# Moving mixer A's heads up behind their query jobs, and gathering the products with the values of mixers B and C

## The chip, the cores and the metric

One core of a Trainium2 chip runs the whole program. The metric is the device time of one execution in microseconds; the kernel before takes 1936.8 us (median of 3 runs, 1934.24 to 1936.91).

## The reference, cut to what matters

Two layers run over two sequences with shared weights, a "prompt" of 512 tokens (p) and a "sample" of 1024 tokens (s), all float32, 1024 channels:

```
even layer:  h = rmsnorm(x)*(1+scale)+shift;  q,k,v,gates = split(h @ w_in_ab)
  A: 8 query heads on 2 key heads, RMS norm and rotary on q and k, dense softmax over all keys
  B: 8 heads, softmax over three dilated sliding windows, mixed by their log-sum-exp
  x += gate * rmsnorm(concat(A*silu(ga), B*silu(gb)) @ w_out_ab)
odd layer:   the same frame around w_in_cd, w_out_cd
  C: 12 heads, each query sees a window of 8 x 16 neighbours on a 64-wide grid, learned bias
  D: a real 2-D Fourier transform and a linear map
```

## The kernel before, in words

The sequences are cut into units of 512 tokens: the sample has units 0 and 1, the prompt unit 2. A layer's input projection is split into jobs of 256 columns. For layer 0 they are, in order, `kva` (keys and values of A), `qa0`, `qa1` (queries of A's heads 0 to 3 and 4 to 7), `kb0`, `qb0`, `vb0`, `kb1`, `qb1`, `vb1` (mixer B), and four gate jobs `ga0` to `gb1` (list in `run`, line 1271). A job multiplies in three float32r passes (high and low halves), norms and rotates on VectorE, ScalarE and GpSimd, and leaves a closure `finish` in `self.late`; `flush` runs it in the middle of a later job: 4 transposes on TensorE for each 128 columns, then a spill to DRAM (`q0s`, `k0s`). The attention functions load queries, keys and values back from DRAM. All DMAs are issued on one queue, that of SyncE (SP), which issues in order.

The line order of the program is only a priority. The program is built with a planner (`schedule_with_timeline_sim=True`, line 1396) that lists the instructions of each engine in an order of its own, by an estimate of when each is ready. So the projection's matrix products of later jobs fill in where attention waits. That order is then fixed: on the chip every engine runs its list in order.

Mixer A (`attn_a`, L683) runs for one key head, 4 query heads, at a time. In the kernel before both calls stand after job `kb0` (lines 1300 to 1303). With the first of them `self.idle` turns false, and from then on the `finish` transposes take their PSUM bank from the three of the projections (`pD`) instead of the two that attention transposes into (`pT`).

Mixer B works on pairs of heads (`attn_b_pair`, L768) for 512 queries: four softmax steps for both heads, then `out_b` (L821) for each head. Mixer C works on one head and 512 queries (`attn_c_unit`, L1049) in four windows. Each head's end in B and C is a *unit* here, and has the same pieces: transposes of the probabilities on TensorE into a `pT` bank (L147), a copy of the bank to SBUF (`copy_pt`, L664, in turn on ScalarE and VectorE, into two tags of two buffers, so four copies can be held), and products with the values (`pv2`, L670), which take 64 of the array's columns: product number n writes the upper or the lower half of the bank `po`, by n odd or even. `fold` adds the halves. In the kernel before each bank's products follow its copy in program order.

- C, sample: 24 units of 4 banks, 3 products each; C, prompt: 12 units of 4 banks, 2 products each.
- B, sample: 16 units with banks of 3, 3, 4, 4 products; B, prompt: 8 units with 3, 3, 4.

A float32 product is recorded as two matmuls, so that C of the sample has 24 x 12 x 2 = 576 records.

Of the kernel before, what the change touches and what calls it, by code (L numbers as in the profile page):

```python
# [18 lines left out]
P = 128  # L19
# [103 lines left out]
class Body:  # L123
# [537 lines left out]
    def copy_pt(self, pt, nm, w=512, rows=P):  # L661
        self.np += 1
        t = self.sb.tile([P, 512], F32, tag="pt" + "hl"[self.np % 2], name="ptc" + nm, bufs=PTB)
        (self.nc.vector.tensor_copy if self.np % PTD == 0 else self.nc.scalar.copy)(t[:rows, :w], pt[:rows, :w])  # L664
        return t

    def pv2(self, out, v, p, n):

        x = 64 * (n % 2)
        self.nc.tensor.matmul(out[x:x + HD], v, p, start=n < 2, stop=False, tile_position=(0, x), skip_group_check=True)  # L670

    def fold(self, po, nm, w=512, view=None):

# [147 lines left out]
    def out_b(self, g, h, pr, x, ev, V1, V2, nm):  # L821
        hf = g.hf
        po = self.pO(f"o{nm}")

        for gi in range(2):
            pt = self.pT(f"pt1{nm}{gi}")
            for i, (t, j) in enumerate(((0, 0), (0, 1), (1, 0), (1, 1))):
                self.tr(pt[:, i * P:(i + 1) * P], ev[2 * gi + t][:, j * P:(j + 1) * P])
            ph = self.copy_pt(pt, f"1{nm}{gi}")
            for j, t, cnt, b in ((0, 0, 1, 0), (1, 0, 2, 1), (2, 1, 1, 3)):  # L830
                t += 2 * gi
                self.pv2(po[:, t * P:(t + cnt) * P], V1[2 * gi + j], ph[:, b * P:(b + cnt) * P], j if gi == 0 else 2 + j)

        pc = po.rearrange("p (t r a) -> p r t a", t=4, r=4)
        for kt in range(hf):
            pt = self.pT(f"pt2{nm}{kt}")
            for t in range(4):
                self.tr(pt[:, t * P:(t + 1) * P], ev[t][:, 256 + kt * P:256 + (kt + 1) * P])
            p2 = self.copy_pt(pt, f"2{nm}{kt}").rearrange("p (t r a) -> p r t a", t=4, r=4)
            for r in range(4):  # L840
                self.pv2(pc[:, r], V2[r * hf + kt], p2[:, r], 2 + r)
        of = self.fold(po, nm, view=lambda v: v.rearrange("p (t r a) -> p r t a", t=4, r=4))
        self.dma(self.md[0, g.name, pr][HD * x:HD * x + HD, 512 * h:512 * h + 512], of)

# [204 lines left out]
    def attn_c_unit(self, g, h, head):  # L1049

        nc, pool = self.nc, self.sb
        n, S, nh = g.name, g.S, g.nhalf
        nrow = 12 if nh == 2 else 8
        NG = nrow // 4
        pr, hh = head // 2, head % 2
        nm = f"c{n}{head}{h}"

        T = self.l1.tile([P, nrow, 32], F32, tag="bt", name="T" + nm, bufs=2)
        r0 = 1 + 4 * h if nh == 2 else 5
        src = self.bias_dr[:, head, r0:r0 + nrow, :]  # L1060
        self.dma(T, bass.AP(src.tensor, src.offset, [[32, 8], [NCH * 24 * 32, 16], [1, 32 * nrow]]))
        T = T[:, ::-1, :]
        K0 = 4 * h * GRID
        ksrc = self.kd[1, n, pr][:, :, K0:K0 + nrow * GRID]
        km = self.load_k(ksrc, HD * hh, nrow * GRID, nm, *((self.l1, "kc") if hh else ()))
        q = self.load_q(self.qd[1, n, pr], HD * hh, h, nm)
        if hh == 0:
            vsrc = self.vd[1, n, head // 4][pr % 2]
            self.vt = []
            for i in range(4):  # L1070
                c0, c1 = max(16 * i - 8, 0), min(16 * i + 24, GRID)
                V = pool.tile([P, NG, P], F32, tag="V", name=f"V{nm}{i}", bufs=VB)
                self.dma(V[0:4 * (c1 - c0)], vsrc[:, c0:c1, h:h + NG].rearrange("r c g d -> r c (g d)"))
                self.vt.append(V)
        Vs = [V[:, :, HD * hh:HD * hh + HD] for V in self.vt]
        if nh == 2:
            TT = self.l1.tile([P, nrow, 32], F32, tag="btr", name="TT" + nm, bufs=1)
            nc.gpsimd.tensor_add(TT, T, self.mrow[:, h, :].unsqueeze(2).to_broadcast([P, nrow, 32]))
            T = TT
        bias = {}  # L1080
        for kind, wo, w in ((0, 8, 24), (1, 0, 32), (2, 0, 24)):
            b = self.l1.tile([P, nrow, w], F32, tag="bias", name=f"bi{nm}{kind}", bufs=BB)
            nc.gpsimd.tensor_add(b, T[:, :, wo:wo + w], self.mcol[:, kind, wo:wo + w].unsqueeze(1).to_broadcast([P, nrow, w]))  # L1083
            bias[kind] = b
        po = self.pO("o" + nm)
        k3 = km.rearrange("p (r c) -> p r c", c=GRID)
        for i in range(4):
            c0, c1 = max(16 * i - 8, 0), min(16 * i + 24, GRID)
            w = c1 - c0
            W, kw = nrow * w, 4 * w  # L1090
            b = bias[(0, 1, 1, 2)[i]]
            e = pool.tile([P, 1024], F32, tag="e", name=f"e{nm}{i}", bufs=EB)[:, 0:W]
            ps = self.pS(f"s{nm}{i}")[:, 0:W]
            self.qk(ps.rearrange("p (r c) -> p r c", c=w), q, slice(P * i, P * i + P), k3[:, :, c0:c1])
            m = pool.tile([P, 1], F32, tag="nmax", name=f"m{nm}{i}", bufs=4)
            nc.vector.tensor_tensor_reduce(out=e, in0=ps, in1=b.rearrange("p r w -> p (r w)"), scale=1.0,  # L1096
                                           scalar=-3.0e38, op0=ALU.add, op1=ALU.max, accum_out=m)
            ngm = pool.tile([P, 1], F32, tag="nmx2", name=f"ngm{nm}{i}", bufs=4)
            nc.vector.tensor_scalar_mul(ngm, m, -0.125)  # L1099
            den = pool.tile([P, 1], F32, tag="den", name=f"den{nm}{i}", bufs=4)  # L1100
            nc.scalar.activation(e, e, AF.Exp, bias=ngm, scale=0.125, accum_out=den)  # L1101
            rd = pool.tile([P, 1], F32, tag="rd", name=f"rd{nm}{i}", bufs=4)
            nc.vector.reciprocal(rd, den)
            nc.vector.tensor_scalar_mul(e, e, rd)
            pt = self.pT(f"pt{nm}{i}")
            for x in range(NG):
                self.tr(pt[:kw, x * P:(x + 1) * P], e[:, x * kw:(x + 1) * kw])
            ph = self.copy_pt(pt, f"{nm}{i}", NG * P, kw)
            for x in range(NG):
                self.pv2(po[:, i * P:(i + 1) * P], Vs[i][:kw, x], ph[:kw, x * P:(x + 1) * P], NG * i + x)  # L1110
        self.dma(self.md[1, n, pr][HD * hh:HD * hh + HD, 512 * h:512 * h + 512], self.fold(po, nm))


# [111 lines left out]
    def run(self):  # L1225
# [4 lines left out]
        with tc.tile_pool(name="l0", bufs=1) as self.l0:  # L1230
# [42 lines left out]
            for g, us in ((gp, [2]), (gs, [0, 1])):  # L1273
                done = []
                if g is gs:
                    self.idle = True
                    done = jobs[3:3 + LEAD0 + LEAD1]
                    for i, kind in enumerate(done[:LEAD0]):
                        if i == SO:
                            H = self.s3_operand(0, 2)  # L1280
                        self.s2_0_job(Hs, [0], kind)
                    self.bias_shift()
                    self.s3(0, 2, "e", H)
                    Hs[1], step = self.s1_steps(0, 1)
                    for kind, i in zip(done[LEAD0:], ST0):
                        step(i[0])
                        self.s2_0_job(Hs, [0], kind)
                        step(i[1])
                for kind in jobs:
                    if g is gp and kind == "ga0":  # L1290
                        Hs[0] = self.s1(0, 0)
                    self.s2_0_job(Hs, [1] if kind in done else us, kind)
                    m = mods.pop(0) if mods else None
                    if end:
                        end()
                    end = self.adaln(*m) if m else None
                    if g is gp and kind == "qa1":
                        self.mb = self.l0.tile([P, 1248], F32, name="mask_b", tag="mask", bufs=1)
                        self.dma(self.mb, self.a["mask_b"])
                    if kind == "kb0":  # L1300
                        self.idle = False
                        self.attn_a(g, 0)
                        self.attn_a(g, 1)
                    elif kind == "vb0":
                        self.attn_b(g, 0, 0)
                    elif kind == "vb1":
                        self.attn_b(g, 0, 1)
                        if g is gs:
                            self.attn_b(g, 1, 0)
                            self.attn_b(g, 1, 1)  # L1310
# [89 lines left out]
```

## Time and profile before

| what | value |
|---|---|
| runs | 1936.8, 1936.91, 1934.24 us |
| the profiled execution | 1936.24 us, its span 1934.2 us |
| TensorE busy | 1857.0 us (96%) |
| VectorE, ScalarE, GpSimd busy | 1195.3, 927.1, 591.4 us |
| granted TensorE clock, mean | 0.988 |

The span is the time from the first to the last instruction; 2 us of the execution lie around it. A matmul's end is modelled and matmuls overlap, so a busy share near 100% does not show how closely they follow one another: the distance from one start to the next does. The stages on the span, read from which matmuls run when: layer 0 of the prompt to 310 us, projections of the sample with little attention from 310 to 520, mixer A of the sample from 520 to 960 and its mixer B to 1228, layer 1 with C of the prompt from 1365 and C of the sample from 1485 to 1820, then the last output projection.

### The profile page before, as it was taken

To read this page: it belongs to the slowest core of one execution; us is meant where nothing else is said; L and a number is where in the kernel's file an instruction comes from. 1 tells how busy PE (TensorE), PEld (TensorE's weight loads), DVE (VectorE), ACT (ScalarE), POOL (GpSimd) and SP (SyncE) were. 2 spreads that over 40 slices of the span, in tenths; PEclk is the share of its full clock that TensorE was granted. 3 is DMA by queue.
4 is the path that set the end of the run, shared out by engine and by line. 5 is a ranking of instruction groups with operands and counts; after the bars stand their busy time and mean duration, and the time that the engine had idled before them with its cause. 6 is when DMAs were issued, how large, how long until landed. Compare 5 with 4: busy or idle time off the path is not lost. (4 is left out here: it accounts for less than half of the span.)

```text
span 1934.2 us, 37850 instructions
## 1 busy us (share of the span) xinstructions
PE 1857.0 (96%) x13752; PEld 1614.9 (83%) x13752; DVE 1195.3 (62%) x3110; ACT 927.1 (48%) x2197; POOL 591.4 (31%) x534
## 2 busy tenths in 40 slices
PE   6999999999999999999999989799999999998998
PEld 4789768999998988889977667788887888887898
DVE  2688863254767666767765677564566544668733
ACT  3456543343356554555554555453554433445531
POOL 3631224354722121121101121353433323335310
PEclk9999999999999999999999999899999999999999
DMA  9754445467763323244344563654677664668643
GB/s 303 253 175 147 126 138 184 126 197 224 231 207 112 104 93 108 64 135 145 116 146 150 182 193 113 205 181 136 216 233 224 195 180 150 200 206 267 221 156 142
DMA packets 255353, 333.03 MB, mean 172 GB/s; under 512 B 25672, under 2 KB 172456, under 8 KB 255168
## 3 DMA queue, kind: packets, MB, share of 16 engines
q1 hardware_dynamic: 255168, 330.62, 54.4%
q8 instruction: 108, 1.77, 0.4%
q14 instruction: 77, 0.63, 0.1%
HBM read 248.68 MB, written 81.87 MB: 171 GB/s over the span
## 5 line engine op out<-in xcount | busy, mean ns | idle before, releaser
L143 PE MATMUL y<-who,hhm 128*128 128x256 f32 x768 | 219.9, 288 | 13.0 <-ACT hhm L891 13.0
L143 PE MATMUL y<-who,hlm 128*128 128x256 f32 x768 | 218.6, 288 | 2.9 <-DVE hlm L892 2.9
L143 PE MATMUL y<-wlo,hhm 128*128 128x256 f32 x768 | 218.6, 287 | 0.2 <-DVE wlo L386 0.2
L143 PEld LDWEIGHTS y<-who,hhm 128*128 128x128 f32 x768 | 148.1, 193 | 16.6 <-ACT hhm L891 14.1
L143 PEld LDWEIGHTS y<-who,hlm 128*128 128x128 f32 x768 | 147.6, 193 | 5.4 <-DVE hlm L892 3.9
L143 PEld LDWEIGHTS y<-wlo,hhm 128*128 128x128 f32 x768 | 148.2, 194 | 1.8 <-issue 1.4
L717 ACT ACTIVATE eas<-sas,nmas 128x512 f32<-128x512 f32 x128 | 86.8, 684 | 69.9 <-DVE nmas L713 69.6
L1083 POOL TENSOR_TENSOR bics<-TTcs,mkc 128x288 f32<-128x288 f32 (+1 forms) x72 | 65.5, 911 | 127.7 <-DVE mcs L1096 108.1
L654 DVE TENSOR_TENSOR ptlas<-ptas,pthas 128x512 fp32r<-128x512 f32 x128 | 85.7, 685 | 19.6 <-ACT pthas L652 18.8
L386 POOL TENSOR_TENSOR wlo<-wso,who 128x512 fp32r<-128x512 f32 x40 | 55.9, 1400 | 132.4 <-ACT who L385 106.5
L708 DVE TENSOR_REDUCE mxas<-sas 128x1 f32<-128x512 f32 x128 | 86.3, 683 | 12.7 <-PE sas L143 12.2
L652 ACT CAST pthas<-ptas 128x512 fp32r<-128x512 f32 x128 | 70.5, 590 | 29.1 <-PE ptas L147 25.7
L143 PE MATMUL t1v<-wh1v,hh 128*128 128x256 f32 x288 | 82.2, 286 | 0.0
L143 PE MATMUL t1v<-wh1v,hl 128*128 128x256 f32 x288 | 82.0, 285 | 0.0
L143 PE MATMUL t1v<-wl1v,hh 128*128 128x256 f32 x288 | 81.9, 285 | 0.0
L1101 ACT ACTIVATE ecs<-ecs,ngmcs 128x288 f32<-128x288 f32 (+1 forms) x96 | 54.8, 571 | 56.3 <-DVE ngmcs L1099 54.8
L914 ACT ACTIVATE ysq<-y 128x256 f32<-128x256 f32 x96 | 36.6, 382 | 87.7 <-PE y L143 70.6
L147 PE MATMUL ptas<-ident,eas 128*128 128x128 f32 x512 | 76.6, 273 | 0.3 <-DVE eas L725 0.3
L143 PE MATMUL oas<-pthas,Vas 128*128 128x256 f32 x256 | 68.9, 285 | 0.0
L143 PE MATMUL oas<-ptlas,Vas 128*128 128x256 f32 x256 | 68.5, 294 | 0.2 <-DVE ptlas L654 0.2
L891 ACT CAST hhm<-og 128x512 fp32r<-128x512 f32 x48 | 29.7, 619 | 75.4 <-POOL og L890 46.1
L385 ACT CAST who<-wso 128x512 fp32r<-128x512 f32 x80 | 48.7, 616 | 35.3 <-PE y L143 10.8
(628 smaller groups left out, 6317.2 us busy)
## 6 DMA issues: line engine op xcount, KB each, us to landing
wso<-w_out_ab SPq DMA_DIRECT2D x48, 256.0 KB
kcs<-k1s SPq DMA_DIRECT2D x24, 384.0 KB
wso<-w_out_cd SPq DMA_DIRECT2D x32, 256.0 KB
ws1k<-w_in_cd SPq DMA_DIRECT2D x28, 256.0 KB
wskb<-w_in_ab SPq DMA_DIRECT2D x24, 256.0 KB
wsqb<-w_in_ab SPq DMA_DIRECT2D x24, 256.0 KB
wsvb<-w_in_ab SPq DMA_DIRECT2D x24, 256.0 KB
ws1q<-w_in_cd SPq DMA_DIRECT2D x24, 256.0 KB
```

What stands on the lines that cost most here:

```text
L143: self.nc.tensor.matmul(out, l, r, start=start, stop=stop, skip_group_check=True)
L147: self.nc.tensor.transpose(out, in_, self.ident[:k, :k])
L385: nc.scalar.copy(hi, st)
L386: (nc.vector if c in dve else nc.gpsimd).tensor_sub(lo, st, hi)
L652: nc.scalar.copy(h[:rows, :w], pt[:rows, :w])
L654: nc.vector.tensor_sub(lo[:rows, :w], pt[:rows, :w], h[:rows, :w])
L708: nc.vector.tensor_reduce(mx[:, c:c + 1], ps, op=ALU.max, axis=AX.X, negate=True)
L717: nc.scalar.activation(e[:, 512 * c:512 * c + 512], pss[c], AF.Exp, bias=nmx, accum_out=den[:, c:c + 1])
L891: nc.scalar.copy(hh, t)
L914: nc.scalar.activation(sq[:, 0:256], ps[:, t], AF.Square, accum_out=ss[j][:, job:job + 1])
L1083: nc.gpsimd.tensor_add(b, T[:, :, wo:wo + w], self.mcol[:, kind, wo:wo + w].unsqueeze(1).to_broadcast([P, nrow, w]))
L1101: nc.scalar.activation(e, e, AF.Exp, bias=ngm, scale=0.125, accum_out=den)
```

## The change

Three edits. `attn_a(g, 0)` now follows job `qa0` and `attn_a(g, 1)` follows `qa1`, each behind a `flush` that runs the job's own `finish`; `self.idle` turns false after `qa0`. In `out_b` and `attn_c_unit` all transposes and copies of a unit come first, then all its products. `together` adds a wait of the first product for the last copy, and an order without a wait from each product to the next.

```diff
     def copy_pt(self, pt, nm, w=512, rows=P):
...
+        self.copied = (self.nc.vector.tensor_copy if self.np % PTD == 0 else self.nc.scalar.copy)(t[:rows, :w], pt[:rows, :w])
+    def together(self, ms):
+        self.after(ms[0], self.copied)
+        for a, b in zip(ms, ms[1:]):
+            self.after(b, a, False)
 # out_b
-            ph = self.copy_pt(pt, f"1{nm}{gi}")
-            for j, t, cnt, b in ((0, 0, 1, 0), (1, 0, 2, 1), (2, 1, 1, 3)):
-                t += 2 * gi
-                self.pv2(po[:, t * P:(t + cnt) * P], V1[2 * gi + j], ph[:, b * P:(b + cnt) * P], j if gi == 0 else 2 + j)
+            p1.append(self.copy_pt(pt, f"1{nm}{gi}"))
...
+        for gi in range(2):
+            for j, t, cnt, b in ((0, 0, 1, 0), (1, 0, 2, 1), (2, 1, 1, 3)):
+                t += 2 * gi
+                ms.append(self.pv2(...))
+        for kt in range(hf):
             for r in range(4):
-                self.pv2(pc[:, r], V2[r * hf + kt], p2[:, r], 2 + r)
+                ms.append(self.pv2(pc[:, r], V2[r * hf + kt], p2[kt][:, r], 2 + r))
+        self.together(ms)
 # attn_c_unit
-            ph = self.copy_pt(pt, f"{nm}{i}", NG * P, kw)
+            pts.append((self.copy_pt(pt, f"{nm}{i}", NG * P, kw), kw))
+        for i, (ph, kw) in enumerate(pts):
             for x in range(NG):
-                self.pv2(po[:, i * P:(i + 1) * P], Vs[i][:kw, x], ph[:kw, x * P:(x + 1) * P], NG * i + x)
+                ms.append(self.pv2(...))
+        self.together(ms)
 # run
-                    if kind == "kb0":
+                    if kind[:2] == "qa":
+                        self.flush()
                         self.idle = False
-                        self.attn_a(g, 0)
-                        self.attn_a(g, 1)
+                        self.attn_a(g, int(kind[2]))
```

## Rows read from the trace of the kernel before

**Rows 1.** The page, part 1: busy us, share of the span, instructions.
```profile
PE 1857.0 (96%) x13752; PEld 1614.9 (83%) x13752; DVE 1195.3 (62%) x3110; ACT 927.1 (48%) x2197; POOL 591.4 (31%) x534
```
**Rows 2.** Busy time by stage: PE, PEld, DVE, ACT, POOL, clock, DMA share, GB/s.
```profile
310.00:520.00 210.00, 208.07 (x1721) 201.28 (x1719) 100.18 (x217) 82.82 (x179) 107.04 (x84) 1.00 0.61 193
960.00:1100.00 140.00, 139.14 (x1131) 103.59 (x1129) 89.07 (x237) 68.88 (x150) 19.70 (x15) 1.00 0.49 154
1100.00:1228.00 128.00, 116.65 (x1135) 95.23 (x1135) 90.88 (x233) 62.72 (x152) 27.07 (x24) 0.97 0.54 163
1485.00:1742.00 257.00, 255.03 (x1712) 215.33 (x1711) 140.52 (x443) 104.14 (x253) 81.66 (x85) 1.00 0.64 191
1742.00:1820.00 78.00, 67.83 (x539) 60.36 (x540) 62.59 (x164) 42.59 (x112) 36.25 (x31) 0.93 0.78 246
```
**Rows 3.** The waits of PE from 1740 to 1820: total us, times, longest us.
```profile
PE ocs L670 <- ACT ptccs L664: 3.3, 1, 3.3
```
**Rows 4.** Timeline of PE: start us, us, instruction, merged count; two runs of products and what follows.
```profile
1401.11 0.44 PE L670 MATMUL ocp<-ptccp,Vcp 128*64 128x128 f32 x4
1401.48 0.42 PE L147 MATMUL ptcp<-ident,ecp 128*96 128x128 f32 x2
...
1659.98 0.88 PE L670 MATMUL ocs<-ptccs,Vcs 96*64 96x128 f32 x12
1660.79 0.66 PE L147 MATMUL ptcs<-ident,ecs 128*128 128x128 f32 x4
1661.20 0.42 PE L143 MATMUL scs<-kcs,qhcs 128*128 128x384 f32 x1
```
**Rows 5.** Timeline of PE: projections ahead of a run, and transposes that follow no run.
```profile
1665.35 0.40 PE L143 MATMUL c1g<-hh,wh1g 128*128 128x512 f32 x1
1665.58 0.40 PE L143 MATMUL c1g<-hl,wh1g 128*128 128x512 f32 x1
1665.90 0.88 PE L670 MATMUL ocs<-ptccs,Vcs 128*64 128x128 f32 x12
...
1220.96 0.60 PE L147 MATMUL pt2bs<-ident,ebs 128*128 128x128 f32 x4
1221.32 0.36 PE L143 MATMUL y<-who,hlm 128*128 128x256 f32 x1
```
**Rows 6.** The first and the last run of products on PE's timeline.
```profile
205.20 0.65 PE L670 MATMUL obp<-ptc1bp,V1bp 128*64 128x128 f32 x6
...
1819.90 0.65 PE L670 MATMUL ocs<-ptccs,Vcs 96*64 96x128 f32 x6
```
**Rows 7.** Busy time of L670 alone (PE, PEld), in three of these stages.
```profile
960.00:1100.00 140.00, 16.15 (x196) 11.80 (x196) 1.00 0.49 154
1100.00:1228.00 128.00, 20.51 (x252) 15.20 (x252) 0.97 0.54 163
1485.00:1742.00 257.00, 32.43 (x432) 23.73 (x432) 1.00 0.64 191
```
**Rows 8.** Timeline of PE: the last transposes of unit 0's `qa0`, the sample's and the prompt's first scores.
```profile
491.04 0.66 PE L147 MATMUL qTqa<-ident,qtqa 128*128 128x128 f32 x4
...
520.18 0.50 PE L143 MATMUL sas<-kas,qhas 128*128 128x512 f32 x1
...
98.78 0.71 PE L143 MATMUL sap<-kap,qhap 128*128 128x512 f32 x2
```
**Rows 9.** Timeline of SP's queue: that unit's spill, a weight load, query loads; the prompt's load.
```profile
497.51 0.46 SPq L140 DMA_DIRECT2D q0s<-spqa  x1
498.06 0.73 SPq L140 DMA_DIRECT2D wskb<-w_in_ab  x1
503.95 0.52 SPq L140 DMA_DIRECT2D qhas<-q0s  x1
...
95.07 0.54 SPq L140 DMA_DIRECT2D qhap<-q0p  x1
```
**Rows 10.** Timeline of DVE: one copy of a transposed bank.
```profile
1661.48 0.55 DVE L664 COPY ptccs<-ptcs 96x384 f32<-96x384 f32 x1 [1.67 <-PE ptcs L147]
```

More of the change, by code (lines that the diff above doesn't have):

```diff
@@ L663, in copy_pt @@
         t = self.sb.tile([P, 512], F32, tag="pt" + "hl"[self.np % 2], name="ptc" + nm, bufs=PTB)
-        (self.nc.vector.tensor_copy if self.np % PTD == 0 else self.nc.scalar.copy)(t[:rows, :w], pt[:rows, :w])
+        self.copied = (self.nc.vector.tensor_copy if self.np % PTD == 0 else self.nc.scalar.copy)(t[:rows, :w], pt[:rows, :w])
         return t
+    def together(self, ms):
+        self.after(ms[0], self.copied)
+        for a, b in zip(ms, ms[1:]):
+            self.after(b, a, False)
     def pv2(self, out, v, p, n):
         x = 64 * (n % 2)
-        self.nc.tensor.matmul(out[x:x + HD], v, p, start=n < 2, stop=False, tile_position=(0, x), skip_group_check=True)
+        return self.nc.tensor.matmul(out[x:x + HD], v, p, start=n < 2, stop=False, tile_position=(0, x),
+                                     skip_group_check=True)
     def fold(self, po, nm, w=512, view=None):
@@ L823, in out_b @@
         po = self.pO(f"o{nm}")
+        p1, p2, ms = [], [], []
         for gi in range(2):
@@ L838, in out_b @@
                 self.tr(pt[:, t * P:(t + 1) * P], ev[t][:, 256 + kt * P:256 + (kt + 1) * P])
-            p2 = self.copy_pt(pt, f"2{nm}{kt}").rearrange("p (t r a) -> p r t a", t=4, r=4)
+            p2.append(self.copy_pt(pt, f"2{nm}{kt}").rearrange("p (t r a) -> p r t a", t=4, r=4))
+        for gi in range(2):
+            for j, t, cnt, b in ((0, 0, 1, 0), (1, 0, 2, 1), (2, 1, 1, 3)):
+                t += 2 * gi
+                ms.append(self.pv2(po[:, t * P:(t + cnt) * P], V1[2 * gi + j], p1[gi][:, b * P:(b + cnt) * P],
+                                   j if gi == 0 else 2 + j))
+        for kt in range(hf):
             for r in range(4):
-                self.pv2(pc[:, r], V2[r * hf + kt], p2[:, r], 2 + r)
+                ms.append(self.pv2(pc[:, r], V2[r * hf + kt], p2[kt][:, r], 2 + r))
+        self.together(ms)
         of = self.fold(po, nm, view=lambda v: v.rearrange("p (t r a) -> p r t a", t=4, r=4))
@@ L1085, in attn_c_unit @@
         po = self.pO("o" + nm)
+        pts, ms = [], []
         k3 = km.rearrange("p (r c) -> p r c", c=GRID)
@@ L1107, in attn_c_unit @@
                 self.tr(pt[:kw, x * P:(x + 1) * P], e[:, x * kw:(x + 1) * kw])
-            ph = self.copy_pt(pt, f"{nm}{i}", NG * P, kw)
+            pts.append((self.copy_pt(pt, f"{nm}{i}", NG * P, kw), kw))
+        for i, (ph, kw) in enumerate(pts):
             for x in range(NG):
-                self.pv2(po[:, i * P:(i + 1) * P], Vs[i][:kw, x], ph[:kw, x * P:(x + 1) * P], NG * i + x)
+                ms.append(self.pv2(po[:, i * P:(i + 1) * P], Vs[i][:kw, x], ph[:kw, x * P:(x + 1) * P], NG * i + x))
+        self.together(ms)
         self.dma(self.md[1, n, pr][HD * hh:HD * hh + HD, 512 * h:512 * h + 512], self.fold(po, nm))
```

## The prediction

> **What bounds the kernel now.** I read the page first. TensorE is busy for 96% of the span, and no other engine for more than 62% [rows 1]; the clock column of the stages shows 1.00, its level of 2.4 GHz, but for the starving ones below (0.97 and 0.93) [rows 2]. The table by stage comes next, since the share is a mean: in the stretches where projections fill in behind attention, 960 to 1100 and 1485 to 1742, TensorE is never free (139.14 of 140 us, 255.03 of 257), while at the end of layer 0's attention and of layer 1's it is not (116.65 of 128, 67.83 of 78) [rows 2]. There the projections have run out and the attention's own chain sets the pace; a wait seen there is that of a product for the copy of its bank, 3.3 us [rows 3]. So I count in two kinds of stage: *filled* ones, where a microsecond off TensorE's list is a microsecond off the time, and *starving* ones, where it need not be. VectorE is at 140.52 of 257 us in the filled stage of mixer C [rows 2], so it doesn't take over as the bound. Last, the timeline of TensorE, to price what is regrouped.
>
> **Gathering the products.** A run of 4 records lasts 0.37 us to the next instruction, one of 12 lasts 0.81 [rows 4]. That is 0.44 for 8 more records, or 0.22 for each pair of products with alternate halves, and a fixed 0.15 for the run (0.37 - 0.22). Going in costs more: a projection's matmul takes 0.23 before the next of its kind and 0.32 before a run [rows 5], so 0.09. Coming out too: four transposes behind a run take 0.41 [rows 4], four that follow other transposes 0.36 [rows 5], so 0.05. A run therefore costs 0.29 us beside its products (0.15 + 0.09 + 0.05).
>
> Counting unbroken stretches of L670 on TensorE's timeline gives 137 runs, the first and the last as shown [rows 6]: 51 in C of the sample, 30 in C of the prompt, 40 and 16 in B of the sample and of the prompt. After the change there is one for each unit: 24, 12, 16, 8, in all 60. Savings: C sample 27 runs, 7.8 us; C prompt 18, 5.2; B sample 24, 7.0; B prompt 8, 2.3. In C of the sample a run that holds an odd number of three-product banks leaves one product without a partner; there are 18 such runs (12 of 6 records, 6 of 18), 9 more partnerless steps than 24 full runs of 6 pairs have (153 against 144), 9 x 0.22 = 2.0 us. Sum 24.3 us.
>
> How much of it lies on the path? All 5.2 us of C prompt (its stage has fill throughout); of C sample's 9.8 us the share of its records in the filled stage, 432 of 576 [rows 7], 7.4; of B sample's 7.0 the share 196 of 448 (16 units x 28 records) [rows 7], 3.1. Together 15.7 us. The other 8.6 (24.3 - 15.7) lie in starving stages, among them, as I take it without a row, all 2.3 of B prompt.
>
> What the gathering adds: the first product waits for the last copy, 0.55 us on VectorE [rows 10]. Behind it on TensorE's list stand the transposes and scores of the next windows, and for those VectorE and ScalarE wait. In a filled stage the planner puts projections between (the c1g matmuls of [rows 5] are such), which hide it; in a starving one it can cost up to 0.55 in each of the some 23 units there (8 of B prompt, 9 of B sample by 252 of 448 records, 6 of C by the 144 of 576 left [rows 7]), 12.7 us. Against it stand the 8.6 us of saving that I didn't count. I take the two as nothing together; the ends are 8.6 us gained and 12.7 lost.
>
> **Moving the heads.** The matmuls, loads and spills of mixer A stay the same in number; only their place in the program changes, past `qa1` and `kb0`. For the prompt little can move: its first scores follow their own query load by 3.7 us already (95.07 to 98.78) [rows 8, 9], so I take nothing, with one such trip either way as the ends. For the sample, the first heads need the keys, which are there, and unit 0's `qa0`, whose last transposes are at 491.04; its first scores stand at 520.18 [rows 8], behind all of `qa1`. SP issues the second spill at 497.51 and the query load at 503.95 [rows 9]. If the load stays there and scores follow it by the prompt's 3.7 us, they begin at 507.7, some 13 us earlier; without the trip the bound would be 29 us (520.18 - 491.04), and none if the planner leaves the list as it is.
>
> What is that worth? `qa1`'s products become fill, so nothing is lost from TensorE's list. When the fill runs out, attention is 13 us further on. A pair of B's heads (56 records) takes 40 us in the filled stage (140 / (196/56)) and 28.4 in the starving one (128 / (252/56)) [rows 7]: 13/40 x 28.4 = 9.2 us less of the starving stage. Bounds: 21 us (29/40 x 28.4), and below nothing a loss of 10: between 498.79 and 503.95 SP issues nothing [rows 9], and if the earlier load holds up the weights queued behind it for such 5.2 us in both units, TensorE has only those projections there (208.07 of 210 us busy [rows 2]). The flush gives qa1's transposes a bank of the projections instead of the attention's; under 1 us, counted as nothing.
>
> **Sum.** 15.7 + 9.2 = 24.9 us. The profiled execution took 1936.24 us, 2 us more than its span and 0.6 below the median of the runs: 1936.2 - 24.9 = 1911 us.
>
> **Rivals.**
> *The copies set the pace.* In every starving unit the run waits out its last copy, and nothing of the 8.6 us comes in: 15.7 - 12.7 + 9.2 = 12.2 us are left, 1924 us. For it: the one wait of 3.3 us [rows 3]. Against: in the filled stage it is the copy that waited for TensorE, 1.67 us [rows 10]. A rule speaks for this rival: by the Trainium skill, TensorEngine Tiling (Array Packing), PSUM Bottleneck, tiling speeds up TensorE but not the emptying of PSUM, and the copy out of it may become the bottleneck. The trace shows that in one place alone, the wait just named.
> *Handed back in mixer C.* The planner sees a shorter run and puts more projections between two units; they run out earlier and 1742 to 1820 starves for as long as was saved. For it: attention has priority and fill takes what is left. Against: TensorE was the late one there, as in the same row. Left are 3.1 + 9.2: 1924 us.
> *Not one run.* The order carries no adjacency; other work may stand between the products, and the runs stay as many. Then only the heads count: 1927 us. Against: all of a unit's products are ready once its last copy is.
> *Everything counts.* Starving stages profit as well and the heads gain their bound: 24.3 + 21 = 45.3 us, 1891 us. For it: the starving stages are a chain of TensorE pieces. Against: the query trip [rows 9].
> *Slower: the four copies.* A unit now holds its three or four copies until its run, so the other unit's copies wait for that run. Price where it is on the loop of a pair of B's heads: a run of 8 steps, 0.15 + 8 x 0.22 = 1.9, its way in 0.1, a copy 0.55, eight transposes 0.7 (twice the 0.36), 3.3 us. In the starving stages there are 8.5 such pairs (4 + 4.5), 28 us, and 6 units of C at 1.5 + 0.1 + 0.55 + 0.5 = 2.65, 16 us. All of it: 1936.2 - 24.9 + 44 = 1955 us. It decides from 29 us on, two thirds of that. Against: the next pair's first steps need only the buffers that the first head's transposes free.
>
> **How the numbers follow.** This measurement tells 0.2%, about 3.9 us, from no change. Chances: forecast 0.42 (own range 1900 to 1922), copies 0.09, handed back 0.12, not one run 0.08, everything 0.15, slower 0.14. Of the second to fourth 0.07 fall within 0.2%. Faster 0.42 + 0.15 + 0.22 = 0.79, same 0.07, slower 0.14. The range 1886 to 1942 leaves out most of the slower case (0.11) and an end of the best (0.04).
>
> **What would show it.** Runs of L670: 60, of 24 records in C sample and 28 in B sample. The sample's first scores near 507 instead of 520. A shorter stretch between the run-out of fill (1100) and the last product of B. In the filled stage of C a unit takes some 0.4 us less (9.8/24). The prediction is wrong if the runs stay over 100, if first scores don't move, or if VectorE's e tiles of mixer B wait for the first head's run.

## The result: 21 us slower, and the profile after

The changed kernel takes 1956.8 us (median of 4, 1951.87 to 1959.1) beside 1935.5 us for the kernel before (median of 4): a ratio of 1.0108, 95% interval 1.0085 to 1.0131, or 21 us slower. Forecast were 1911 us, with a range of 1886 to 1942. The profiled execution took 1951.87 us, its span is 1949.7. One execution of the kernel before_vfold below, at 2573 us with a granted clock of 0.65, was in a slower state and is left out of every number.

The page, part 1 (busy us, share of the span, instructions), answers to [rows 1]; then the stages of [rows 2] (PE, PEld, DVE, ACT, POOL, clock, DMA share, GB/s); then the products alone, now at L676, in the three stages of [rows 7].

```profile
PE 1848.7 (95%) x13752; PEld 1619.3 (83%) x13752; DVE 1193.5 (61%) x3110; ACT 925.0 (47%) x2197; POOL 592.2 (30%) x534
```
```profile
310.00:520.00 210.00, 206.66 (x1718) 200.97 (x1717) 102.60 (x218) 82.45 (x180) 101.74 (x80) 1.00 0.59 191
960.00:1100.00 140.00, 140.00 (x1111) 108.51 (x1111) 81.08 (x223) 64.98 (x138) 17.97 (x14) 1.00 0.48 146
1100.00:1228.00 128.00, 114.15 (x1090) 91.35 (x1089) 83.72 (x217) 60.81 (x147) 24.79 (x20) 0.96 0.52 160
1485.00:1742.00 257.00, 253.25 (x1768) 217.21 (x1767) 155.18 (x490) 111.64 (x277) 88.83 (x92) 1.00 0.64 197
1742.00:1820.00 78.00, 65.66 (x488) 59.43 (x487) 62.15 (x158) 39.64 (x101) 37.13 (x31) 0.85 0.76 238
```
```profile
960.00:1100.00 140.00, 11.76 (x168) 10.32 (x168) 1.00 0.48 146
1100.00:1228.00 128.00, 15.69 (x224) 13.75 (x224) 0.96 0.52 160
1485.00:1742.00 257.00, 31.18 (x456) 25.03 (x456) 1.00 0.64 197
```

TensorE is busy for less time (1848.7 us, 1857.0 before), yet the span grew by 15.5 us: what was added is time in which it stands, 101.0 us in all instead of 77.2. Mixer B shows it first. From 960 to 1228 it gets 392 records done (168 + 224) where it did 448 [rows 7], although its attention began earlier; mixer C gets more done than before (456 against 432).

The gathering itself is there: 60 runs, in the sample 24 of 24 records each in C and 16 of 28 in B. TensorE's timeline (start us, us, instruction, merged count), answering to [rows 4]:

```profile
1651.42 1.53 PE L676 MATMUL ocs<-ptccs,Vcs 96*64 96x128 f32 x24
1663.02 1.53 PE L676 MATMUL ocs<-ptccs,Vcs 96*64 96x128 f32 x24
1664.49 0.55 PE L147 MATMUL ptcs<-ident,ecs 128*128 128x128 f32 x3
```

A run of 24 lasts 1.47 us to the next instruction, against two of 12 at 0.81 [rows 4]. The units follow each other by 11.6 us; before, the second run of a unit came every 12.5 us (1647.48 to 1659.98, the later of them in [rows 4]).

The heads moved as well. The last transposes of unit 0's `qa0`, the sample's first scores, and SP's queue with the second spill and the query load, answering to [rows 8, 9]:

```profile
491.15 0.60 PE L147 MATMUL qTqa<-ident,qtqa 128*128 128x128 f32 x4
...
511.69 0.63 PE L143 MATMUL sas<-kas,qhas 128*128 128x512 f32 x2
```
```profile
499.13 0.37 SPq L140 DMA_DIRECT2D q0s<-spqa  x1
499.59 0.42 SPq L140 DMA_DIRECT2D wskb<-w_in_ab  x1
...
505.67 0.52 SPq L140 DMA_DIRECT2D qhas<-q0s  x1
```

The scores start 8.5 us earlier (520.18 before), not 13. And there is something that no step of mine had: in the prompt, behind `qa1`, TensorE stands. First the stretch 80 to 100 before, the same after, then TensorE's timeline after (in brackets the idle time ahead of an instruction and what ended it):

```profile
80.00:100.00 20.00, 18.52 (x143) 16.94 (x143) 18.77 (x37) 10.23 (x23) 20.00 (x15) 1.00 0.57 179
```
```profile
80.00:100.00 20.00, 7.91 (x48) 6.47 (x47) 17.94 (x35) 6.36 (x16) 18.09 (x13) 0.67 0.55 170
```
```profile
82.42 0.28 PE L143 MATMUL tqa<-wlqa,hh 128*128 128x256 f32 x1
82.54 0.28 PE L143 MATMUL tqa<-whqa,hl 128*128 128x256 f32 x1
82.75 1.02 PE L143 MATMUL adg<-mod,sel 128*2 128x512 f32 x2
83.70 0.66 PE L147 MATMUL qTqa<-ident,qtqa 128*128 128x128 f32 x4
85.54 0.66 PE L147 MATMUL qTqa<-ident,qtqa 128*128 128x128 f32 x4 [1.18 <-DVE qtqa L489]
97.10 1.09 PE L147 MATMUL qTqa<-ident,qtqa 128*128 128x128 f32 x4 [10.90 <-DVE qtqa L489]
97.84 0.56 PE L143 MATMUL tkb<-whkb,hh 128*128 128x256 f32 x1
98.20 0.42 PE L143 MATMUL tkb<-wlkb,hh 128*128 128x256 f32 x1
98.41 0.41 PE L143 MATMUL tkb<-whkb,hl 128*128 128x256 f32 x1
```

The transposes of `qa1` stand on TensorE's list ahead of `kb0`'s products (`tkb`) and wait 10.9 us for `qa1`'s norms on VectorE. Before, `kb0`'s 96 `tkb` records ran from 85.25 to 98.31. The products that follow come 0.21 us apart instead of the 0.12 between products of the same shape just ahead of the wait. The granted clock of the 20 us, 0.67, is a mean over both of its levels (1.2 and 2.4 GHz): it is 1.00 from 80 to 86, 0.54 in the wait from 86 to 97, and still 0.50 from 97 to 100.

### The profile page after: what moved, and what is told of

It reads as the page before. It is cut to its first block, busy times and chain, and to the rows that moved or that the text cites. A ratio compares the mean times of both kernels' runs of the same rounds, so it can differ in the third digit from the quotient of the medians.

```text
span 1949.7 us, 37814 instructions
## 1 busy us (share of the span) xinstructions
PE 1848.7 (95%) x13752; PEld 1619.3 (83%) x13752; DVE 1193.5 (61%) x3110; ACT 925.0 (47%) x2197; POOL 592.2 (30%) x534
## 4 chain that ended last, share of the span: by engine, by line
PE 76%; DMA 10%; DVE 7%; issue 2%; POOL 2%; ACT 1%; SPq 1%; POOLq 0%; ACTq 0%; DVEq 0%
PE y L143 9%; PE c1q L143 5%; PE c1g L143 5%; PE c1k L143 5%; PE t1v L143 5%; PE tvb L143 4%; PE ggb L143 3%; PE oas L143 3%; PE tqb L143 3%; PE sas L143 3%; PE gga L143 3%; PE ptas L147 3%; PE tkb L143 3%; PE tkva L143 2%; DMA Vcs<-v1s 1%
## 5 line engine op out<-in xcount | busy, mean ns | idle before, releaser
L143 PEld LDWEIGHTS y<-who,hhm 128*128 128x128 f32 x768 | 148.9, 194 | 14.4 <-ACT hhm L903 12.7
L903 ACT CAST hhm<-og 128x512 fp32r<-128x512 f32 x48 | 29.6, 618 | 80.2 <-DVE og L902 45.2
L385 ACT CAST who<-wso 128x512 fp32r<-128x512 f32 x80 | 48.4, 616 | 37.5 <-issue 12.6
```

The costliest lines, as they stand in the source:

```text
L143: self.nc.tensor.matmul(out, l, r, start=start, stop=stop, skip_group_check=True)
L385: nc.scalar.copy(hi, st)
L903: nc.scalar.copy(hh, t)
```

## The experiments

"B" in the table is the sample's stretch of mixer B, from its first score to its last product; "tail" is from C's last product to the last product of the output projection. Both are starts on TensorE's timeline of the one profiled execution, in us; kernels whose mixer B is the same differ by up to 6 us in it when their heads start alike, so smaller differences say little. Times are medians, ratios those to the kernel before on the same chip. Without a flush the earlier heads lengthen B by 7 us of themselves: in heads_late 864 records of other work go between B's own, before 826.

| kernel | time | ratio, interval | B | tail |
|---|---|---|---|---|
| before | 1932.8 to 1935.5 | 1 | 255.1 | 104.6 |
| the change | 1956.8 | 1.0108 (1.0085 to 1.0131) | 285.4 | 112.4 |
| heads | 1943.3 | 1.0056 (1.0039 to 1.0073) | 262.6 | 104.5 |
| flush_only | 1944.0 | 1.0046 (1.0032 to 1.0061) | 254.8 | 104.8 |
| flush_t | 1937.1 | 1.0020 (1.0008 to 1.0031) | 252.0 | 104.4 |
| heads_tbank | 2006.8 | 1.0385 (1.0364 to 1.0407) | 275.6 | 104.4 |
| heads_split | 1949.1 | 1.0087 (1.0066 to 1.0108) | 270.9 | 104.4 |
| heads_late | 1933.2 | 0.9999 (0.9986 to 1.0011) | 261.9 | 104.4 |
| gather | 1948.9 | 1.0078 (1.0057 to 1.0099) | 272.1 | 111.6 |
| gather_c | 1931.2 | 0.9987 (0.9977 to 0.9998) | 253.8 | 111.8 |
| gather_half | 1938.4 | 1.0033 (1.0019 to 1.0047) | 253.6 | 129.1 |
| gather_five | 1949.8 | 1.0088 (1.0073 to 1.0104) | 267.4 | 110.7 |
| split31 | 1934.9 | 1.0006 (0.9992 to 1.0021) | 252.5 | 112.4 |
| split13 | 1934.2 | 1.0003 (0.9988 to 1.0018) | 257.5 | 111.7 |
| gather_vfold | 1946.0 | 1.0059 (1.0042 to 1.0076) | 263.2 | 103.0 |
| before_vfold | 1952.7 | 1.0099 (1.0080 to 1.0118) | 250.6 | 129.8 |
| both_late | 1951.1 | 1.0086 (1.0069 to 1.0103) | 281.3 | 114.9 |
| c_late | 1931.5 | 0.9989 (0.9977 to 1.0001) | 267.9 | 112.1 |
| halfb_c | 1933.9 | 0.9999 (0.9990 to 1.0008) | 253.4 | 113.3 |
| halfb_c_late | 1928.9 | 0.9976 (0.9962 to 0.9989) | 261.8 | 113.9 |

Each edit also makes the planner order the whole program anew, and that alone can cost as much as what is looked for: before_vfold differs from the kernel before in one line, its B is shorter, and it is 0.99% slower. So a reading below rests on several kernels where it can. All five with one run for each head of B (the change, gather, gather_five, gather_vfold, both_late) are 0.59 to 1.08% slower; the five with two runs are between 0.24% faster and 0.33% slower.

### Which half of the change costs: gather, heads, heads_split, heads_tbank

*gather* is the changed kernel with the heads put back:

```
-                    if kind[:2] == "qa":
-                        self.flush()
+                    if kind == "kb0":
                         self.idle = False
-                        self.attn_a(g, int(kind[2]))
+                        self.attn_a(g, 0)
+                        self.attn_a(g, 1)
```


> Only the products are gathered; mixer A's heads stand behind kb0 as before. My theory now: the 21 us come from the heads' move and the gathering itself saves what I counted in the filled stages, 10 to 16 us, so 1920 to 1927. Rival, the four copies: the gathering is what costs, because a unit holds its copies until its run; then this kernel is 1950 or more and the starving stretch of mixer B (1100 to 1260) is where it is longer. A third reading, gained and given back: 1933 to 1939.

It is 15 us slower (0.78%), so the rival was right that the gathering costs by itself, and in mixer B (272.1 against 255.1 us); its reason, the four copies, is looked at below. My theory at that point, that the heads alone were to blame, fell.

*heads* is the kernel before with that part of the change alone:

```
-                    if kind == "kb0":
+                    if kind[:2] == "qa":
+                        self.flush()
                         self.idle = False
-                        self.attn_a(g, 0)
-                        self.attn_a(g, 1)
+                        self.attn_a(g, int(kind[2]))
```


> Only the heads are moved, with the flush ahead of them; the products stay spread. Theory: all of the loss is here, 1948 to 1960, and TensorE stands for some 11 us between the last product of qa1 and the first of kb0 of the prompt, as after the change (one wait of 10.9 us). Rival, the four copies: 1926 to 1940, since nothing is gathered.

Slower too, by 0.56%, less than either reading of it said; the wait is there (12.2 us in three, the longest 9.2). Two losses, then, not one.

*heads_tbank* differs from heads in one line, *heads_split* in which heads move:

```
# heads_tbank
+                        self.idle = kind == "qa0"
# heads_split
+                    if kind in ("qa0", "kb0"):
+                        if kind == "qa0":
+                            self.flush()
+                        self.idle = False
+                        self.attn_a(g, int(kind == "kb0"))
```


> The heads moved and flushed as in the kernel heads, but the transposes of qa1 take the attention's banks (T) and not the projections' (D), so that the products of kb0 need not come behind them in the ring of three D banks. Theory that the ring makes the 10.9 us: that wait falls below 3 us and the time is at least 8 us below heads, unless the transposes now wait for the first heads in the ring of two T banks (then the first heads of kv 1 come later, and part of it is lost again). Rival, the queue of VectorE: the transposes of qa1 wait for their chain in whatever bank, TensorE's wait stays near 11 us and the time within 4 us of heads.

> The heads of kv 0 follow qa0 with a flush, those of kv 1 follow kb0 as before, so nothing of qa1 is flushed ahead of kb0's products. Theory: the prompt's wait is gone (below 3 us) and the sample's first heads still start near 507; 1926 to 1940. Rival, that moving the first heads is itself harmful (SP's queue and the weights behind the query load): 1944 or more with no wait at 86 to 97.

With T banks the prompt's wait is gone (18.67 us busy from 80 to 100), so it was the bank. But the transposes of `qa1` now stand behind the first heads in the ring of two T banks, as the "unless" had it, and the projections stop behind them: in the sample the transposes run at 685 to 695 us (516.6 to 533.2 before), `kb0`'s last product at 758.4 (606.2 before), and from 560 to 700 TensorE is busy for 109.05 us of 140 (140.00 before). heads_split has no long wait in the prompt (the longest 2.2 us) and is still slower, as its rival said. In the sample it flushes `qa0` in the same way; the stretch 520 to 536 before, after the change and in heads_split, then heads_split's timeline of TensorE:

```profile
520.00:536.00 16.00, 16.00 (x136) 14.52 (x132) 10.45 (x27) 6.36 (x13) 10.12 (x8) 1.00 0.85 284
```
```profile
520.00:536.00 16.00, 13.67 (x80) 9.69 (x79) 13.26 (x29) 7.75 (x17) 9.70 (x8) 0.79 0.43 122
```
```profile
520.00:536.00 16.00, 13.67 (x81) 9.51 (x80) 11.55 (x26) 7.65 (x17) 9.53 (x7) 0.79 0.54 158
```
```profile
526.73 0.87 PE L147 MATMUL ptas<-ident,eas 128*128 128x128 f32 x6 [2.33 <-DVE eas L725]
...
532.59 0.58 PE L143 MATMUL tkb<-whkb,hh 128*128 128x256 f32 x1
```

The longest wait is 2.33 us; the granted clock is 0.83 from 526 to 529 and 0.50 from 529 to 532, and 81 instructions stand where 136 were (not all of the same shapes). `kb0`'s first product comes only at 532.59 (521.2 before). Why heads_split loses as much as 0.87%, more than heads, is not settled by that: B and C are longer in it too.

### The flush by itself: flush_only, flush_t, heads_late

```
# flush_only: the heads stay behind kb0 (without the line self.idle = False: flush_t)
-                    if kind == "kb0":
+                    if kind[:2] == "qa":
+                        self.flush()
+                        self.idle = False
+                    elif kind == "kb0":
...
# heads_late
-                    if kind == "kb0":
+                    if kind in ("qa1", "kb0"):
                         self.idle = False
-                        self.attn_a(g, 0)
-                        self.attn_a(g, 1)
+                        self.attn_a(g, int(kind == "kb0"))
```


> The kernel before with the flush alone: qa0 and qa1 are finished at once, their transposes in the projections' D banks, while the heads stay behind kb0 and the products spread. Theory that the flush and not the heads' new place makes the loss of the kernel heads (10.5 us): TensorE's wait of 9 to 11 us behind qa1 of the prompt is there, and the time is 1939 to 1947. Rival, that the heads' place does it: 1930 to 1937, whatever the wait.

> The same flush alone, with the transposes in the two T banks, which no head uses yet at that point. Theory of the ring of three D banks: the products of kb0 pass the transposes, no wait above 3 us in 80 to 100, and the time is 1930 to 1938. Rival, the chain on VectorE: the transposes of qa1 stop TensorE in whatever bank; a wait of 9 us or more and 1939 to 1947.

> Products as before; no flush: the heads of kv 0 follow qa1 (in which the transposes of qa0 are finished), those of kv 1 follow kb0. Theory of the ring of D banks: without a flush the next projection's products fill behind a query job as before, so TensorE has no wait above 2 us in 80 to 100 and in 490 to 560 and the clock stays at 1.00 there; the time is 1922 to 1937. Rival, that heads ahead of kb0 cost by their place alone: 1942 or more without such waits.

The same 20 us, and TensorE's waits from 80 to 104 (us in total, times, longest), first of flush_only, then of flush_t:

```profile
80.00:100.00 20.00, 7.76 (x45) 6.25 (x44) 16.86 (x32) 5.87 (x14) 17.81 (x13) 0.73 0.53 171
```
```profile
PE qTqa L147 <- DVE qtqa L489: 12.2, 3, 9.6
```
```profile
80.00:100.00 20.00, 19.07 (x145) 17.10 (x144) 19.57 (x38) 10.54 (x23) 20.00 (x14) 1.00 0.59 187
```
```profile
PE qTqa L147 <- DVE qtqa L489: 0.5, 2, 0.3
```

No head has moved in these two, and only the bank differs. The flush in D banks costs 0.46%, 8.9 us; in T banks 0.20%, 3.9 us, with the wait gone. The 5 us between them are the ring's (the intervals don't overlap): the three D banks are handed out in program order, two of them to transposes that can't start yet, and `kb0`'s products come behind. By the order in which the program takes D banks the third is that of `adg`, which VectorE reads late in flush_only:

```profile
90.77 0.67 DVE L262 TENSOR_TENSOR mob<-adg,mob 2x512 f32<-2x512 f32 x1
```

From there on it is the order of TensorE's list, with the transposes (96.82) ahead of `kb0`'s first product (97.56), that holds the product up. The Trainium skill, Perfetto Trace Analysis, Optimizing Tensor Performance, Matmuls, says that independent groups of matmuls should rotate through different PSUM banks, so that the emptying of one overlaps the next group. This trace shows a case that the sentence leaves out: the banks did rotate, one tenant was not ready, and the next group stood for 9.6 us. What the other 0.20% of flush_t is stays open.

The heads' own place can be read from heads beside flush_only, which has the same flush: 0.56 and 0.46%, and the intervals overlap.

heads_late has the earlier heads without a flush: no price (0.9999). Its heads do run earlier, first scores of the sample at 514.0 and B's last product at 1218.8 instead of 1225.9, 7 us; but a time that is not shorter means that these are not kept to the end. Its heads do not stand where those of the change stand, and heads_split, where the first of them do, loses 0.87%: that the place costs nothing holds for heads_late and, beside the flush, for heads.

### The gathering by itself: gather_c, gather_half, gather_five

```
# gather_c: out_b as in the kernel before; attn_c_unit gathers
# gather_half, attn_c_unit (out_b alike, behind each second copy)
+            if i % 2:
+                for c in (i - 1, i):
+                    ...
+                self.together(ms)
+                ms = []
# gather_five, copy_pt
-        t = self.sb.tile([P, 512], F32, tag="pt" + "hl"[self.np % 2], name="ptc" + nm, bufs=PTB)
+        t = self.sb.tile([P, 512], F32, tag="pt" + "hl"[self.np % 2], name="ptc" + nm, bufs=PTB + self.np % 2)
... (two other uses of the tag ptl name its third buffer too)
```


> Products gathered in mixer C alone; mixer B and the heads as before. From the kernel gather: mixer B's stretch of the sample (first score to last product) grew from 255 to 272 us, a unit of C fell from 12.5 to 11.6 us, and behind C's last product 111.6 us are left instead of 104.6. Theory that mixer B makes the loss: B's stretch is back at 255 +- 3, C's sample stretch is some 10 us shorter, the tail gives up to 7 us back; 1923 to 1933 beside a kernel before of 1933. Rival, that C loses as well (a starving end that grows by more than the 10 us): 1938 or more.

> Both mixers gather, but in two runs for each unit, one behind each pair of copies, so that a unit holds two copies and not four. Theory of the four copies (a unit that holds all four buffers keeps the next one's copies, transposes and e tiles waiting): mixer B's stretch of the sample is 262 us or less (272 in gather, 255 before) and the time 1925 to 1938. Rival, that any gathering slows mixer B by taking products away from where they filled TensorE between two pairs: the stretch stays at 268 or more and the time at 1943 or more.

> As gather, with a third buffer in the tag of a unit's first and third copy: five copies can be held, so the next unit's first copy needs no run ahead of it. Theory of the four copies: a good part of the 17 us that mixer B's stretch grew is back, 255 to 264 us, and the time 1930 to 1941. Rival, that the run's wait for its last copy or the missing products between two pairs cost it: the stretch stays at 268 to 276, the time 1944 to 1952.

gather_c is 0.13% faster, and B is back: the loss is mixer B's. Gathering in C does shorten it, from its first prompt score to its last product 490.6 us instead of 501.6, and then gives 7 of these 11 back in the tail. The output projection's tile `y` alone, in the 78 us up to C's last product and behind it (after the length: TensorE's busy time and records, its loads, VectorE and ScalarE on that tile, clock, DMA share, GB/s), of the kernel before, gather_c and gather_half:

```profile
1742.00:1820.30 78.30, 40.62 (x280) 36.54 (x280) 4.13 (x10) 4.70 (x20) 0.93 0.78 246
1820.30:1934.00 113.70, 104.66 (x872) 104.36 (x872) 32.27 (x50) 18.02 (x76) 0.98 0.48 163
```
```profile
1727.00:1805.40 78.40, 37.17 (x240) 33.00 (x240) 3.32 (x8) 3.79 (x16) 0.91 0.77 245
1805.40:1926.00 120.60, 110.45 (x912) 109.31 (x912) 33.09 (x52) 18.95 (x80) 0.98 0.46 159
```
```profile
1723.00:1801.70 78.70, 18.87 (x129) 16.98 (x129) 1.23 (x3) 1.88 (x8) 0.96 0.74 237
1801.70:1940.00 138.30, 124.04 (x1023) 122.62 (x1023) 35.14 (x57) 20.77 (x88) 0.98 0.50 169
```

A C that ends sooner has had less of `y` between its units: 872 products are left behind it before, 912 with one run, 1023 with two. That work is only moved; C's end is not the kernel's end.

gather_half brings B fully back (253.6), yet it is 0.33% slower, with the tail just shown. gather_five takes ScalarE's wait for a free copy buffer (6.6 us in gather, shown below) away; B falls by 4.7 us and the time does not. Two theories were left: the copies held, and the work that remains behind the last copy.

### What it is in mixer B: split31, split13, gather_vfold, before_vfold

Two cuts of a head's products into two runs, 20 + 8 and 6 + 22 records:

```
+            if n in (hf, 1 + hf):        # split13: (0, 1 + hf)
+                for f, i in todo:
+                    f(i)
+                self.together(ms)
...
```


> As gather, but in mixer B a head's products go in two runs, the first behind the third copy (20 records), the second behind the fourth (8). Theory of the tail (what counts is how much is left behind the last copy, since the next pair's scores stand behind it on TensorE): mixer B's stretch of the sample is 253 to 260 us as with halves (253.6), the time 1928 to 1938. Theory of the held copies (three are held until the first run): 262 to 270 us, and the same as in split13.

> As split31 with the cut elsewhere: the first run behind the first copy (6 records), the second behind the fourth (22). As many runs, as many copies held. Theory of the tail: mixer B's stretch is 264 to 272 us, near gather's 272, and the time 1942 to 1950. Theory of the held copies: 262 to 270 us in both, within 4 us of each other.

Both theories missed. The tail theory wanted split13 near 272, the buffer theory both at 262 to 270; both are near 255, and their times are the kernel before's within the interval. What goes with B's stretch is a wait of ScalarE: at `fold` it stands until a head's run has ended, with the exponentials of the next windows behind it on its list. From 967 to 1245 (us in total, times, longest), of before and of gather; then VectorE's wait for the scores in the same stretch, which is looked at below:

```profile
ACT ofbs L679 <- PE obs L670: 13.6, 10, 3.9
...
DVE ebs L853 <- PE sbs L805: 12.1, 15, 2.4
```
```profile
ACT ofbs L686 <- PE obs L676: 28.6, 15, 4.6
...
ACT ptc1bs L664 <- PE obs L676: 6.6, 7, 3.5
...
DVE ebs L865 <- PE sbs L812: 32.8, 19, 4.2
```

ScalarE's wait at `fold` is 33.9 us in gather_five, 11.0 in split31, 19.6 in split13.

So I moved the first step of `fold` to VectorE, with and without the gathering:

```
-        nc.scalar.copy(dst[HD:P], lo)
+        nc.vector.tensor_copy(dst[HD:P], lo)
```


> As gather, but the fold's first step (a copy of the bank's lower half) is on VectorE, which waits for the run there anyway with the second step; ScalarE then waits for no run's end. Theory of ScalarE's stand: mixer B's stretch of the sample falls from 272 to 262 us or less and the time by 8 us or more below gather, to 1930 to 1940. Rival, that the wait only goes with a chain that is longer for another reason: the stretch stays at 267 or more (VectorE stands instead), the time at 1943 to 1952.

> The control: the kernel before with the fold's first step on VectorE. Theory of ScalarE's stand: little to take back here (13.6 us of waits), mixer B's stretch 250 to 258 us, the time 1928 to 1938. Rival, that the fold's place alone is worth something, gathering or not: 1925 or less, or, if VectorE becomes late, 1940 or more.

B falls by 8.9 us with gathering and by 4.5 without, to 263.2 and 250.6: 12.6 of the 17 us between them remain, and the time of gather_vfold, 1946.0, is in the rival's range. Now VectorE stands at the same place:

```profile
DVE ofbs L686 <- PE obs L676: 20.1, 10, 3.4
```

ScalarE's stand is at most a part. before_vfold missed its expectation by 15 us; it shows once more that an earlier end of C (1809 instead of 1820) can go with a later end of the kernel: its tail is 129.8 us.

The traces hold one thing more, which sets the kernels with one run apart from the others. With one run for each head, the second head's run mostly stands on TensorE's list between the scores of the next pair, and VectorE waits for the rest of these. In gather (TensorE, then VectorE):

```profile
1149.82 0.64 PE L812 MATMUL sbs<-kbs,qbs 64*32 64x256 f32 x8
1150.38 1.09 PE L676 MATMUL obs<-ptc1bs,V1bs 128*64 128x128 f32 x12
1151.30 1.04 PE L676 MATMUL obs<-ptc2bs,V2bs 128*64 128x128 f32 x16
1152.27 0.64 PE L812 MATMUL sbs<-kbs,qbs 64*32 64x256 f32 x8
...
1152.96 0.69 DVE L865 CUSTOM_DVE_ANT_1 ebs<-sbs,mask_b 128x512 f32<-128x512 f32 x1 [3.74 <-PE sbs L812]
```

The run takes 1.89 us there (1150.38 to 1152.27). In the table, a run counts as between scores if TensorE does a score right before and right after it; VectorE's waits (in total, 967 to 1245) are those for scores and, where it does the fold's first step, those for the run:

| kernel | B | runs between scores: number, us | VectorE's waits |
|---|---|---|---|
| gather | 272.1 | 7, 13.6 | 32.8 |
| gather_five | 267.4 | 6, 11.3 | 27.6 |
| gather_vfold | 263.2 | 4, 7.6 | 6.0 + 20.1 |
| split13 | 257.5 | 3, 4.4 | 18.7 |
| before | 255.1 | 3, 1.8 | 12.1 |
| gather_half | 253.6 | 1, 1.0 | 10.4 |
| split31 | 252.5 | 2, 1.2 | 9.0 |
| before_vfold | 250.6 | 2, 1.2 | 5.5 + 6.9 |

The change (7 runs, 13.2 us, a wait of 29.6) and both_late (7, 13.2, 26.2) are like gather. No kernel here moves the run or the scores alone, so this goes with the loss and isn't shown to be its cause. How the 17 us are made up is plain from TensorE's record of B's stretch, of before and of gather (columns as in [rows 2]):

```profile
970.80:1225.90 255.10, 244.76 (x2203) 189.51 (x2202) 170.56 (x452) 124.03 (x284) 43.74 (x37) 0.99 0.51 158
```
```profile
967.50:1239.60 272.10, 252.14 (x2202) 197.21 (x2202) 166.36 (x452) 124.77 (x284) 43.00 (x37) 0.94 0.47 148
```

The instructions are as many; TensorE stands for 20.0 us instead of 10.3, and is busy for 7.4 us more at a lower granted clock.

### Put together: both_late, c_late, halfb_c, halfb_c_late

both_late is the changed kernel with heads_late's lines in `run`; c_late is gather_c with them; halfb_c takes out_b from gather_half, attn_c_unit from the change and the heads from the kernel before; halfb_c_late is halfb_c with heads_late's lines.

> The change without its flush: products gathered in B and C, the heads of kv 0 behind qa1, of kv 1 behind kb0. If flush and gathering are two separate losses, about 11 and 16 us, this kernel has the gathering's alone: 1943 to 1951, with mixer B's stretch of the sample near 272 us. Rival, that earlier heads give the longer stretch of B room, so that both together cost less: 1930 to 1940.

> What cost nothing, together: products gathered in mixer C alone, heads of kv 0 behind qa1 without a flush. If the two small gains (0.13% and 0.01%) add up: 1928 to 1932, 0.1 to 0.3% under the kernel before. If the earlier heads' 7 us at the end of layer 0 come through as well: 1922 to 1928. Rival, given back in C's tail: 1933 to 1937.

> Two runs in mixer B (behind each pair of copies), one in mixer C, heads as before. If B's stretch stays at 254 us and C saves as in gather_c, with some 12 fewer runs in B besides: 1926 to 1932, the least so far. Rival, given back in C's tail like the rest: 1932 to 1937.

> The same with the heads of kv 0 behind qa1 and no flush. If the earlier heads' 7 us at the end of layer 0 stay: 1922 to 1929. Rival, that they are given back behind mixer C as in heads_late and c_late: 1929 to 1936.

Without the flush the change costs what the gathering costs alone (0.86% beside 0.78%): the two losses are separate, and nearly add up (0.46 + 0.78 = 1.24, measured 1.08). halfb_c_late is the one kernel that is clearly below the kernel before: 0.24% (0.11 to 0.38), 4.6 us, the best of the 18 that were tried. halfb_c alone gained nothing, c_late 0.11% with an interval that takes in no change. Why the earlier heads pay here, and not in heads_late, is open.

## Why the prediction was wrong

- **The count and price of the runs held.** 137 became 60, a run of 24 lasts the 1.47 us that the prices give (0.15 + 6 x 0.22), and a unit of C got shorter in the filled stage, by 0.9 us (0.4 forecast); of that some 0.7 are projections that no longer go between two units (32 `c1g` records for each, 35 before, 0.23 us apiece [rows 5]), which leaves 0.2 for the gathering, half of the forecast.
- **The step that failed first: "I take the two as nothing together".** What the gathering adds was priced as one copy's wait, 0.55 us in a unit, bounded by 12.7 us. It costs 15 us by itself, and the sample's mixer B alone grew by 17. The wait was named rightly ("Behind it on TensorE's list stand the transposes and scores of the next windows, and for those VectorE and ScalarE wait"), but the run's own length, 1.9 us for a head in one piece, was left out of its price (the rival *the four copies* had it in): VectorE's wait for scores went from 12.1 to 32.8 us. Shown is that one run for a whole head makes the loss, and that two runs, wherever cut, take it back. By what path one run is so much worse than two is not shown; the runs that stand between scores go with it best.
- **The rival *the four copies*** had the place right, B's pairs, but not the sizes: 28 us for B of both sequences, where the sample's grew by 17 and the prompt's by 3 (124.2 to 127.5), and 16 us in C, which did not come. Its cause finds little support: ScalarE waited 6.6 us for a free copy buffer, and a fifth buffer took that away and left 267.4 us. What was held against it was misread too: by the program the next pair's first step already writes an e tile of either head, so that it needs the second head's transposes as well.
- **Filled stages are no refuge.** From 960 to 1060 TensorE is busy for all of the 100 us in gather too, and yet it does 112 records of products there (118 before) and starts its fourth pair 97.8 us after the first (87.7 before). The longer chain shows as projections put in earlier, and is paid where they have run out: from 1060 to 1250 TensorE is busy for 160.05 us in gather and 167.82 before. I had counted the two kinds of stage apart; a chain that lengthens in the one is paid in the other.
- **The rival *handed back in mixer C* was right** in part: of 11 us in C 7 came back, but in the tail and not in the stage that I named, and with fewer projections between two units (32, 35 before), not more.
- **The second step that failed: the flush, "under 1 us, counted as nothing", and for the prompt "I take nothing".** I saw that the flush changes the bank and did not ask who takes the next bank of that ring. It costs 8.9 us by itself, some 5 of them by the bank that the transposes take; in the prompt TensorE stands for 10.9 us in one wait. The row that warned of it was there: the 20 us from 80 to 100 before, 18.52 busy with `kb0` on TensorE and VectorE at 18.77.
- **Moving the heads.** The first scores came 8.5 us earlier, not 13: the query load is at 505.67, behind two spills, and the scores 6.0 us behind it instead of 3.7. Without the flush 7.1 us of it stand at the end of layer 0's attention, near the 9.2 forecast; in the time nothing is left (0.9999). That the 9.2 came near was in part luck: the 40 and 28.4 us of a pair are misread, since 960 lies 10.8 us ahead of B's first score and a pair's products stand at its end. The first scores of the pairs follow one another by 25.6 to 34.0 us up to 1091 and by 29.2 to 33.9 behind it, no less where TensorE starves. Of the 10 us for SP's held queue these runs tell nothing sure: heads_late loses nothing, and the loss of heads_split is open.

By terms: forecast were 15.7 + 9.2 us gained; measured are 15 lost by the gathering, 9 by the flush and nothing that is clear of the intervals by the heads' place, 24 us beside the 21 of both together.

## What to carry to other kernels

Ask of each edit that moves a use of a rotating buffer who is next in that ring, and what the new tenant waits for: work that could have run stands behind it. Where a planner fills with other work, a full engine does not show that a chain got longer; look at how far the chain is when the filler runs out, and at how much filler is left behind the last piece. Before short instructions are gathered, ask what will stand behind the gathered run on its engine's list, and who waits for that: here two runs for a head cost little or nothing, one run cost 15 us.

## What was not expected of the hardware

The price of a wait on TensorE is more than the wait: behind 10.9 us of idling the 128x256 products came 0.21 us apart instead of 0.12 at a granted clock of 0.50, and a stretch of 16 us in the sample whose longest wait was 2.33 us had a granted clock of 0.79 (1.00 before). Over the sample's mixer B, 20.0 us of standing instead of 10.3 went with a granted clock of 0.94 instead of 0.99.
